# Three output tiles ahead of the last gate, and the first norm's squares on one engine

## The chip, the cores and the metric

The program runs on one core of a Trainium2 chip. The metric is the device time of one execution in microseconds (us), lower is better. The core's engines are named as in the profile: PE is TensorE's matmul, PEld its weight load, DVE is VectorE, ACT is ScalarE, POOL is GpSimd, and SP issues DMAs.

## The reference, cut to what matters

The program is a two-layer decoder trunk over 512 tokens of width 1024. Layer 0 has a recurrent block, layer 1 sparse attention; each is followed by a gated FFN with a small convolution. The change is in layer 0's recurrent block and in the norm before it:

```python
h = h + rglru_mixer(rmsnorm(h, lru_norm_g[j]), lru_w_in[j], ...)

def rmsnorm(x, g):
    y = x * lax.rsqrt(jnp.mean(x * x, axis=-1, keepdims=True) + EPS)
    return y * g

def rglru_mixer(x, w_in, conv_w, conv_b, gate_w, gate_b, a_param, w_out):
    y_br, x_br = jnp.split(x @ w_in, 2, axis=-1)      # each 1280 wide
    y_br = jax.nn.gelu(y_br)
    xc = causal_dwconv(x_br, conv_w, conv_b)          # width 4
    r_gate, i_gate = sigmoid(xc in 10 blocks of 128 @ gate_w + gate_b)
    a = jnp.exp(-LRU_C * r_gate * softplus(-a_param))
    b = sqrt(1 - a * a) * i_gate * xc
    h_t = a_t * h_(t-1) + b_t                         # a scan over tokens
    return (h * y_br) @ w_out
```

## The kernel before, in words

Activations lie with channels on the partitions and the 512 tokens along the row, so `x` is 8 tiles of 128x512 float32. Each matrix product is made of three matmuls (`mm3`, L214 to L216): an operand is split into a rounded high part and a low rest, and high by high, high by low and low by high are added up in one PSUM bank. The high half is made by ACT (a copy, `xh`, `whi`, `ch`, `hh`), the low half by DVE (a subtraction, `xl`, `wlo`, `cl`, `hl`). A weight tile is 128x1024 and 512 KB. Weight tile i goes through the pool `wx`, which has one buffer (tiles `wrawx`, `whix`, `wlox`), where i mod 3 is 2, and else through a pool with two buffers (`wraw`, `whi`, `wlo`). Loads and splits are asked for up to two tiles ahead.

The norm's row scale is applied late: the products run on `x * g`, and what comes out of PSUM is multiplied by `rbc`, the reciprocal root of the mean square, spread over the partitions. Its making has two steps on PE: `norm_finish` sums the squares over the partitions with float32 matmuls of one column (L276), DVE and POOL take the power (`nv`, `rtok`), and `norm_spread` broadcasts it by four more matmuls (L287), which ACT copies to `rbc`. In the kernel before the first three squares of the first norm are made and summed by POOL in a tile `ssum2` (L347, L349), the other five by ACT (L263, L266) and summed by DVE in `ssum` (L267); so `norm_finish` has eight matmuls there, against four in every other norm.

The recurrent block goes over ten blocks n of 128 channels. For each, `project(py, n)` and `project(px, n)` are 24 matmuls each; `yev(n)` and `conv(n)` empty their banks (both multiply by `rbc`); `conv(n)` makes `xr`, one ACT and three DVE taps into `xc`, and the halves `ch` and `cl`; `gate_mm(n)` is six matmuls on these, and `gate_act(n)` its sigmoids. Every two blocks a `burst` of exp, sqrt, gelu, scan and split follows and ends in `hh`, `hl`, the operands of the output product. `newacc` hands out six PSUM banks in turn, `newg` two.

The output product has eight tiles m, each with eight k of 24 matmuls from one weight tile (`lru_oa`) and two last k of six matmuls from a shared one (`lru_ob`). The last gate, `gate_mm(9)`, is tied behind the first short output tiles, which take only k = 0 to 5 until then and k = 6, 7 after it:

```python
            for m in range(2):
                po[m], first[m] = newacc(), self.w()
                outp(po[m], first[m], range(KA - 2))
            gate_mm(NB - 1, self.mm_name)
```

The order of the instructions on each engine comes from a scheduler, which goes by dependencies and priorities; weight splits and `conv` have a raised priority.

Of the kernel before, what the change touches and what calls it, by code (L numbers as in the profile page):

```python
# [10 lines left out]
F32 = mybir.dt.float32  # L11
# [6 lines left out]
NT = 512  # L18
KD = 8
NB = 10  # L20
# [4 lines left out]
RX = 2  # L25
WARM = 10
WLO, QLO, KLO, OLO = True, 'G', 'V', 'V'
KG = 3
NP = 9


# [33 lines left out]
CHP = 150  # L65

START = {1: (1, 0), 3: (0, 1), 4: (1, 1)}
KA, DEF = 8, 6
SLOPE = [2.0 ** (-0.5 * (h + 1)) for h in range(16)]


# [30 lines left out]
class Trunk:  # L102
# [166 lines left out]
    def norm_finish(self, newps):  # L269
        T, V = self.T, self.V  # L270
        ps = newps()
        parts = [self.ssum] + ([self.ssum2] if self.ssum2 is not None else [])
        self.ssum2 = None
        for t in range(4):
            for j, s in enumerate(parts):
                T.matmul(ps[:, t:t + 1], s[:, 128 * t:128 * t + 128], self.cst[:, C_ONE:C_ONE + 1],  # L276
                         start=(j == 0), stop=(j == len(parts) - 1))
        v = self.np_.tile([128, 4], F32, name="nv", bufs=1)
        V.tensor_scalar(v, ps[:, :4], 1.0 / 1024.0, 1e-6, op0=ALU.mult, op1=ALU.add)
        self.rtok = self.np_.tile([128, 4], F32, name="rtok", bufs=1)  # L280
        self.G.tensor_tensor(self.rtok, v, self.mhalf, op=ALU.pow)
# [11 lines left out]
    def start(self):  # L293
        nc, a = self.nc, self.a
        self.prm = self.cp.tile([128, P_END], F32, name="prm")
        self.cst = self.cp.tile([128, C_END], F32, name="cst")
        self.x = [self.cp.tile([128, NT], F32, name=f"x{k}") for k in range(KD)]
        self.plan()
        self.tins, self.tgrp, self.manual = [], None, False
        self.mhalf = self.cp.tile([128, 4], F32, name="mhalf")  # L300
        self.V.memset(self.mhalf, -0.5)
        warm = self.cp.tile([128, 4], F32, name="warm")
        self.S.activation(warm, self.mhalf, AF.Copy)
        self._dma(0)
        self._dma(1)
        self.wd = 2
        nc.scalar.dma_start(self.prm[:, :P_CW], a["prm"][:, :P_CW])
        self._half(0, 0, True)
        for k in range(KD):
            nc.sync.dma_start(self.x[k], a["x"][k])  # L310
            if k in START:
                self._half(*START[k], True)
        nc.sync.dma_start(self.cst, a["cst"])
        nc.sync.dma_start(self.prm[:, P_CW:], a["prm"][:, P_CW:])
        self.ident = self.cst[:, C_ID:C_ID + 128]
# [9 lines left out]
    def run(self):  # L325
        wx = ExitStack()
        extra = lambda: wx.enter_context(self.tc.tile_pool(name="wx", bufs=1))
        self.wx = extra()
        self.warm_up(WARM)
        self.start()  # L330
        st = self.stages
        g0 = {"lru": P_LRUG, "ffn0": P_FFNG, "nsa": P_NSAG, "ffn1": P_FFNG + 8}
        seq = [s for s in ("lru", "ffn0", "nsa", "ffn1") if s in st]
        self.norm_begin(g0[seq[0]])
        self.sq_eng = self.V
        self.ssum2 = self.np_.tile([128, NT], F32, name="rbc", bufs=1)
        for k in range(KD):
            self.norm_split(k)
            if k == 0:
                self._half(0, 0, False)  # L340
            if k in START:
                self._half(*START[k], False)
        self.wsp = 2
        for k in range(KD):
            if k < KG:
                sq = self.ssum2 if k == 0 else self.np_.tile([128, NT], F32, name="sq")
                self.G.tensor_mul(sq, self.x[k], self.x[k])  # L347
                if k > 0:
                    self.G.tensor_add(self.ssum2, self.ssum2, sq)  # L349
            else:  # L350
                self.norm_sq(k, k == KG)
        for s, nx in zip(seq, seq[1:] + [None]):
            self.next_g = g0[nx] if nx else P_FING
            self.next_split = nx is not None
            self.sq_eng = self.G if SSQ[seq.index(s)] else self.V
            if s == "lru":
                self.lru()
            elif s == "nsa":
                wx.close()
                self.spl = 1  # L360
                self.nsa()
                self.wx = extra()
                self.spl = 2
            else:
                self.ffn(int(s[-1]))
        if self.next_split or seq[-1][:3] != "ffn":
            for _ in self.final(slice(0, NT), self.ring(0, 1)):
                pass
        wx.close()
# [36 lines left out]
    def lru(self):  # L406
        S, V, G, T, prm = self.S, self.V, self.G, self.T, self.prm
        with ExitStack() as s:
# [4 lines left out]
            py, px, pg = {}, {}, {}  # L413
# [3 lines left out]
            def project(d, n):  # L417
                d[n] = newacc()
                self.proj(d[n], self.w(), self.xs, range(KD))

            def yev(n):
                y[n] = hp.tile([128, NT], F32R, name=f"hh{n}").bitcast(F32)
                V.tensor_mul(y[n], py[n], self.rbc)

            def conv(n):

                with self.tc.high_priority(offset=CHP):
                    conv_ops(n)
# [29 lines left out]
            def gate_mm(n, after=None):  # L458
                hi, lo = gw.pop(n)
                if n + 1 < NB:  # L460
                    gate_w(n + 1)
                pg[n] = []
                for j in range(2):
                    ps = newg()
                    sl = slice(128 * j, 128 * j + 128)
                    first = self.mm3(ps, hi[:, sl], lo[:, sl], *xcs[n], True, True)
                    if after:
                        self.tc.add_manual_dep(first, after, mybir.DependencyInfo(
                            mybir.DependencyClass.NoSync, mybir.DependencyReason.DATA), reason="output first")
                    pg[n].append(ps)  # L470

            def gate_act(n):
                r[n] = hp.tile([128, NT], F32R, name=f"hl{n}").bitcast(F32)
                ig[n] = p.tile([128, NT], F32, name="ig", bufs=6)
                self.tact(r[n], pg[n][0], AF.Sigmoid, bias=col(P_GB + n))
                self.tact(ig[n], pg[n][1], AF.Sigmoid, bias=col(P_GB + 10 + n))
                u[n] = p.tile([128, NT], F32, name="u", bufs=6)
                self.tact(u[n], r[n], AF.Tanh, scale=self.sp[:, 0, n:n + 1])
                self.G.tensor_mul(ig[n], ig[n], xc[n])
# [42 lines left out]
            def tick():  # L522
                if late:
                    for f in late.pop(0):
                        f()

            def burst(ns):
                at(0, lambda: exps(ns))
                at(1, lambda: sqrts(ns))
                at(2, lambda: gelus(ns))  # L530
                for j, n in enumerate(ns):
                    at(2 + j, lambda n=n: back1(n))
                    at(3 + j, lambda n=n: back2(n))
                    at(4 + j, lambda n=n: back3(n))
# [5 lines left out]
            for k in range(0, KD, 2):  # L540
                for d, w in ((py, w0), (px, w1)):
                    self.proj(d[0], tuple(t[:, 128 * k:128 * k + 256] for t in w), self.xs, range(k, k + 2))
            for n in range(NB):
                if n > 1:
                    project(py, n)
                if n > 0:
                    conv(n - 1)
                if n > 1:
                    gate_act(n - 2)
                    if n - 2 in last:  # L550
                        burst(last[n - 2])
                tick()
                if n > 0:
                    project(px, n)
                if n > 0:
                    gate_mm(n - 1)
                if n == 0:
                    self.norm_finish(newacc)
                    project(py, 1)
                    self.norm_spread(newacc)  # L560
                    self.sp = self.softplus(hp)
                    gate_w(0)
                yev(n)
                tick()

# [14 lines left out]
            po = {}  # L580

            def begin(m):
                po[m] = newacc()
                outp(po[m], self.w(), range(KA))


            first = {}
            for m in range(2):
                po[m], first[m] = newacc(), self.w()
                outp(po[m], first[m], range(KA - 2))  # L590
            gate_mm(NB - 1, self.mm_name)
# [1 line left out]
            burst(last[NB - 1])  # L593
            while late:
                tick()
            for m in range(2):
                outp(po[m], first[m], range(KA - 2, KA), 128 * (KA - 2))
            for m in range(2, DEF):
                begin(m)
            wo = []  # L600
            for m in range(KD):
# [691 lines left out]
```

## Time and profile before

| what | value |
|---|---|
| median of 3 runs | 1320.08 us (1318.04 to 1320.96) |
| profiled execution, its own time | 1320.14 us |
| its span, first to last instruction | 1318.3 us |
| PE busy | 1299.9 us, 99% of the span |
| DVE, ACT, POOL busy | 786.0, 611.4, 248.0 us |
| mean granted TensorE clock | 0.995 of full speed |

The profiled execution's own time is 1.8 us above its span; that part lies outside the instructions. A busy PE is one that has a matmul running: matmuls overlap, so the step from the start of one to the start of the next says more than their duration. The granted clock is 1.00 at 2.4 GHz and 0.50 at 1.2 GHz.

### The profile page before, as it was taken

The numbers are of one execution on the slowest core, as the hardware profiler recorded it, in microseconds if no ns is written. First come the engines' busy times: TensorE is split into PE (matmuls) and PEld (weight loads), VectorE is DVE, ScalarE is ACT, GpSimd is POOL, SyncE is SP. The second block draws the span as 40 slices with busy tenths as digits, with TensorE's granted clock in tenths as the row PEclk, the third lists the DMA queues.
The fourth block names the chain that finished last, engine by engine and source line by source line (L and its number), as shares of the span: only waits on it lengthen the run. The fifth ranks groups of instructions, "written<-read, shape, count | busy, mean of one in ns | idle before, by whom it ended". The sixth has DMA issues, their size and how long they took to land.

```text
span 1318.3 us, 16281 instructions
## 1 busy us (share of the span) xinstructions
PE 1299.9 (99%) x6166; PEld 1064.2 (81%) x6166; DVE 786.0 (60%) x1267; ACT 611.4 (46%) x980; POOL 248.0 (19%) x259
## 2 busy tenths in 40 slices
PE   8999999999999999999999999999999999999997
PEld 6888788888888888888787787888888888888886
DVE  7799765555555533336457978875655555542223
ACT  5789743333333322221348878865433333332220
POOL 2123331000000001115008567643000000000110
PEclk9999899999999999999999999999999999999999
DMA  7222222322222222224231100013222232223221
GB/s 239 91 75 101 77 84 97 98 97 100 96 99 99 98 90 92 94 78 141 96 112 33 34 33 33 17 46 115 97 96 96 96 96 96 96 96 97 96 80 64
DMA packets 36222, 117.71 MB, mean 89 GB/s; under 512 B 4144, under 2 KB 7728, under 8 KB 36144
## 3 DMA queue, kind: packets, MB, share of 16 engines
q1 hardware_dynamic: 34848, 115.61, 26.4%
q8 instruction: 48, 0.79, 0.2%
q10 hardware_dynamic: 1296, 1.07, 0.2%
q14 instruction: 30, 0.25, 0.1%
HBM read 114.57 MB, written 2.10 MB: 88 GB/s over the span
## 4 chain that ended last, share of the span: by engine, by line
PE 91%; DVE 3%; ACT 2%; issue 1%; POOL 1%; DMA 1%; SPq 0%; POOLq 0%; DVEq 0%; ACTq 0%
PE bank L215 27%; PE bank L214 27%; PE bank L216 27%; PE bank L1085 2%; PE bank L1105 1%; PE bank L1101 1%; PE bank L1031 1%; PE bank L1032 1%; PE bank L877 1%; PE bank L835 1%; PE bank L836 1%; PE bank L837 1%; DVE P L1044 0%; PE bank L1104 0%; ACT P L229 0%
## 5 line engine op out<-in xcount | busy, mean ns | idle before, releaser
L214 PE MATMUL bank<-xh,whi 128*128 128x512 f32 x760 | 297.8, 392 | 0.8 <-ACT xh L256 0.2
L215 PE MATMUL bank<-xl,whi 128*128 128x512 f32 x760 | 296.6, 390 | 1.6 <-DVE xl L257 1.6
L216 PE MATMUL bank<-xh,wlo 128*128 128x512 f32 x760 | 296.3, 390 | 1.0 <-DVE wlo L186 0.5
L185 ACT ACTIVATE whi<-wraw 128x1024 fp32r<-128x1024 f32 x143 | 151.2, 1058 | 307.7 <-PE bank L215 252.2
L186 DVE TENSOR_TENSOR wlo<-wraw,whi 128x1024 fp32r<-128x1024 f32 x133 | 164.0, 1233 | 130.5 <-ACT whi L185 120.2
L267 POOL TENSOR_TENSOR ssum<-ssum,sq 128x512 f32<-128x512 f32 x27 | 44.2, 1636 | 771.1 <-issue 581.1
L214 PEld LDWEIGHTS bank<-xh,whi 128*128 128x128 f32 x760 | 142.7, 188 | 33.1 <-DVE nm L1044 0.8
L216 PEld LDWEIGHTS bank<-xh,wlo 128*128 128x128 f32 x760 | 142.6, 188 | 31.8 <-DVE wlo L186 1.0
L215 PEld LDWEIGHTS bank<-xl,whi 128*128 128x128 f32 x760 | 142.7, 188 | 31.7 <-DVE xl L257 3.0
L185 ACT ACTIVATE whix<-wrawx 128x1024 fp32r<-128x1024 f32 x57 | 60.4, 1060 | 138.8 <-PE bank L215 137.2
L215 PE MATMUL bank<-xl,whix 128*128 128x512 f32 x296 | 116.5, 394 | 0.0
L214 PE MATMUL bank<-xh,whix 128*128 128x512 f32 x296 | 116.2, 393 | 0.0
L216 PE MATMUL bank<-xh,wlox 128*128 128x512 f32 x296 | 115.1, 389 | 0.0
L214 PE MATMUL bank<-fh,whi 128*128 128x512 f32 (+1 forms) x272 | 104.0, 382 | 0.0
L215 PE MATMUL bank<-fl,whi 128*128 128x512 f32 (+1 forms) x272 | 103.9, 382 | 0.0
L216 PE MATMUL bank<-fh,wlo 128*128 128x512 f32 (+1 forms) x272 | 103.9, 382 | 0.0
L1061 POOL TENSOR_SCALAR P<-P,c,gtok 128x512 f32<-128x512 f32 (+3 forms) x128 | 79.5, 635 | 100.6 <-DVE c L1057 86.0
L186 DVE TENSOR_TENSOR wlox<-wrawx,whix 128x1024 fp32r<-128x1024 f32 x57 | 69.7, 1222 | 42.5 <-ACT whix L185 42.4
L652 DVE TENSOR_TENSOR ar<-bank,rbc 128x512 f32<-128x512 f32 x48 | 33.2, 691 | 99.2 <-PE bank L216 99.2
L662 DVE TENSOR_TENSOR b<-bank,rbc 128x512 f32<-128x512 f32 x48 | 33.2, 691 | 86.1 <-PE bank L216 86.1
L229 ACT ACTIVATE P<-P,nm 128x512 f32<-128x512 f32 (+3 forms) x128 | 70.9, 556 | 16.8 <-DVE nm L1044 13.7
L229 ACT ACTIVATE t<-t 128x512 f32<-128x512 f32 x48 | 30.4, 632 | 98.0 <-DVE t L658 98.0
(224 smaller groups left out, 2322.8 us busy)
## 6 DMA issues: line engine op xcount, KB each, us to landing
wraw<-in_ffn_in_dram SPq DMA_DIRECT2D x65, 512.0 KB, 3.3
wraw<-in_ffn_out_dram SPq DMA_DIRECT2D x32, 512.0 KB, 3.3
wrawx<-in_ffn_in_dram SPq DMA_DIRECT2D x31, 512.0 KB, 3.2
wrawx<-in_ffn_out_dram SPq DMA_DIRECT2D x16, 512.0 KB, 3.2
wraw<-in_nsa_in_dram SPq DMA_DIRECT2D x16, 512.0 KB, 3.3
wraw<-in_lru_in_dram SPq DMA_DIRECT2D x12, 512.0 KB, 3.6
w<-in_cmp_w_dram SPq DMA_DIRECT2D x8, 512.0 KB, 4.9
wraw<-in_nsa_out_dram SPq DMA_DIRECT2D x8, 512.0 KB, 3.3
```

The lines of the kernel that those rows point to most:

```text
L185: self.S.activation(hi[:, c], raw[:, c], AF.Copy)
L186: (eng or (self.G if self.manual and WLO else self.V)).tensor_sub(lo[:, c], raw[:, c], hi[:, c].bitcast(F32))
L214: ins = mm(ps, wh, xh, start=first, stop=False)
L215: mm(ps, wh, xl, start=False, stop=False)
L216: end = mm(ps, wl, xh, start=False, stop=last)
L229: ins = self.S.activation(out, in_, func, **k)
L267: self.sq_eng.tensor_add(self.ssum, self.ssum, sq)
L652: V.tensor_mul(ar, pa, self.rbc)
L662: V.tensor_mul(b, pb, self.rbc)
L835: T.matmul(pv[t], xh[:, ts], hi[:, sl], start=(k == 0), stop=False)
L1061: G.tensor_scalar(Ps[g, i, br][r], Ps[g, i, br][r], st["c"][:, br, r:r + 1], gtok[:, i, gc:gc + 1], op0=ALU.mult, op1=ALU.mult)
L1085: T.transpose(st["t", kt][:, 128 * r:128 * r + 128], Ps[u][r][:, 128 * kt:128 * kt + 128], self.ident)
```

## The change

It has four parts. The load of weight tile 2 is issued ahead of the loads of `cst` and of the rest of `prm`. All eight squares of the first norm go to ACT and are summed by DVE in `ssum`. The start of the recurrent block is written out: the second `py` projection comes ahead of `norm_finish`, and the second `px` projection is cut in two halves of 12 matmuls with `norm_spread` between them; `gate_mm(0)` comes behind the third `py` projection. Three short output tiles stand ahead of the last gate in place of two, and seven whole ones ahead of the shared weights in place of six, the seventh in a bank of the gate's pair.

```diff
-KA, DEF = 8, 6
+KA, DEF, NE = 8, 7, 3
...
     def norm_finish(self, newps):
...
-        parts = [self.ssum] + ([self.ssum2] if self.ssum2 is not None else [])
-        self.ssum2 = None
         for t in range(4):
-            for j, s in enumerate(parts):
-                T.matmul(ps[:, t:t + 1], s[:, 128 * t:128 * t + 128], self.cst[:, C_ONE:C_ONE + 1],
-                         start=(j == 0), stop=(j == len(parts) - 1))
+            T.matmul(ps[:, t:t + 1], self.ssum[:, 128 * t:128 * t + 128], self.cst[:, C_ONE:C_ONE + 1],
+                     start=True, stop=True)
...
+        self._dma(2)
+        self.wd = 3
         nc.sync.dma_start(self.cst, a["cst"])
...
         for k in range(KD):
-            if k < KG:
-                sq = self.ssum2 if k == 0 else self.np_.tile([128, NT], F32, name="sq")
-                self.G.tensor_mul(sq, self.x[k], self.x[k])
-                if k > 0:
-                    self.G.tensor_add(self.ssum2, self.ssum2, sq)
-            else:
-                self.norm_sq(k, k == KG)
+            self.norm_sq(k, k == 0)
...
+            project(py, 1)
+            self.norm_finish(newacc)
+            px[1], w1 = newacc(), self.w()
+            self.proj(px[1], w1, self.xs, range(KD // 2))
+            self.norm_spread(newacc)
+            self.proj(px[1], tuple(t[:, 64 * KD:] for t in w1), self.xs, range(KD // 2, KD))
+            self.sp = self.softplus(hp)
+            gate_w(0)
+            yev(0)
+            tick()
+            conv(0)
+            yev(1)
+            tick()
+            for n in range(2, NB):
+                project(py, n)
+                if n == 2:
+                    gate_mm(0)
+                conv(n - 1)
...
             def begin(m):
-                po[m] = newacc()
+                po[m] = newg() if m == 6 else newacc()
                 outp(po[m], self.w(), range(KA))
...
-            for m in range(2):
+            for m in range(NE):
                 po[m], first[m] = newacc(), self.w()
                 outp(po[m], first[m], range(KA - 2))
             gate_mm(NB - 1, self.mm_name)
...
-            for m in range(2):
+            for m in range(NE):
                 outp(po[m], first[m], range(KA - 2, KA), 128 * (KA - 2))
-            for m in range(2, DEF):
+            for m in range(NE, DEF):
                 begin(m)
```

## Rows read from the trace of the kernel before

**Rows 1.** The page: busy time, share of the span and instructions.

```profile
PE 1299.9 (99%) x6166; PEld 1064.2 (81%) x6166; DVE 786.0 (60%) x1267; ACT 611.4 (46%) x980; POOL 248.0 (19%) x259
```

**Rows 2.** PE's waits: who waited for whom, total, times, longest.

```profile
PE bank L214 <- ACT ch L443: 1.9, 1, 1.9
PE bank L215 <- DVE xl L257: 1.6, 3, 0.7
```

**Rows 3.** PE's timeline around the last gate: start, us, instruction, idle before.

```profile
142.81 0.40 PE L216 MATMUL bank<-hh,wlo 128*128 128x512 f32 x1
145.10 0.77 PE L214 MATMUL bank<-ch,ghi 128*128 128x512 f32 x1 [1.90 <-ACT ch L443]
146.82 0.80 PE L215 MATMUL bank<-cl,ghi 128*128 128x512 f32 x1 [0.95 <-DVE cl L444]
...
152.30 0.40 PE L216 MATMUL bank<-hh,wlo 128*128 128x512 f32 x1
...
158.59 0.39 PE L216 MATMUL bank<-hh,wlo 128*128 128x512 f32 x1
```

**Rows 4.** Windows around it: busy time, then granted clock, DMA share, GB/s.

```profile
147.00:148.00 1.00, 1.00 (x3) 0.81 (x4) 1.00 (x1) 0.07 (x1) 0.90 (x1) 0.50 0.00 0
...
152.00:153.00 1.00, 1.00 (x6) 0.77 (x6) 0.41 (x1) 1.00 (x2) 0.00 (x0) 1.00 0.00 0
```

**Rows 5.** Groups of instructions, first 30 us: busy, mean ns of one, idle.

```profile
L257 DVE SCALAR_TENSOR_TENSOR xl<-x,prm,xh 128x512 fp32r<-128x512 f32 x8 | 8.5, 1088 | 1.1 <-ACT xh L256 1.0
...
L175 DVE TENSOR_TENSOR wlo<-wraw,whi 128x512 fp32r<-128x512 f32 x4 | 3.6, 893 | 2.9 <-ACT whi L174 2.9
...
L267 DVE TENSOR_TENSOR ssum<-ssum,sq 128x512 f32<-128x512 f32 x4 | 2.7, 680 | 0.0
```

**Rows 6.** DVE's timeline in the first 23 us.

```profile
9.71 3.47 DVE L257 SCALAR_TENSOR_TENSOR xl<-x,prm,xh 128x512 fp32r<-128x512 f32 x2
...
13.71 0.74 DVE L257 SCALAR_TENSOR_TENSOR xl<-x,prm,xh 128x512 fp32r<-128x512 f32 x1
...
19.71 1.22 DVE L186 TENSOR_TENSOR wlox<-wrawx,whix 128x1024 fp32r<-128x1024 f32 x1
```

**Rows 7.** DVE's timeline behind the last gate.

```profile
148.60 0.69 DVE L511 TENSOR_TENSOR hl<-u,hh 128x512 fp32r<-128x512 f32 x1 [0.15 <-ACT hh L510]
152.59 1.23 DVE L186 TENSOR_TENSOR wlox<-wrawx,whix 128x1024 fp32r<-128x1024 f32 x1 [3.30 <-ACT whix L185]
```

**Rows 8.** ACT's timeline behind the last gate.

```profile
151.50 1.06 ACT L185 ACTIVATE whix<-wrawx 128x1024 fp32r<-128x1024 f32 x1 [0.93 <-PE bank L215]
```

**Rows 9.** Chain that ended last: norm sums of the first and second norm.

```profile
20.78 1.68 PE bank L276 x16
...
203.73 0.79 PE bank L276 x8
```

**Rows 10.** POOL's timeline in the first 30 us.

```profile
9.21 3.43 POOL L349 TENSOR_TENSOR rbc<-rbc,sq 128x512 f32<-128x512 f32 x2
```

**Rows 11.** DVE's timeline in the next norm.

```profile
184.18 1.78 DVE L257 SCALAR_TENSOR_TENSOR xl<-x,prm,xh 128x512 fp32r<-128x512 f32 x1
```

**Rows 12.** POOL's timeline in the next norm.

```profile
183.17 3.94 POOL L267 TENSOR_TENSOR ssum<-ssum,sq 128x512 f32<-128x512 f32 x2 [0.60 <-ACT sq L266]
```

**Rows 13.** ACT's timeline in the first 23 us.

```profile
6.71 0.72 ACT L256 ACTIVATE xh<-x,prm 128x512 fp32r<-128x512 f32 x1 [1.62 <-DMA x<-in_x_dram]
...
17.61 0.64 ACT L266 ACTIVATE sq<-x 128x512 f32<-128x512 f32 x1 [1.90 <-DVE ssum L267]
18.15 1.04 ACT L185 ACTIVATE whix<-wrawx 128x1024 fp32r<-128x1024 f32 x1
```

**Rows 14.** ACT's timeline where the first norm's scale comes.

```profile
29.01 0.60 ACT L290 ACTIVATE rbc<-bank 128x512 f32<-128x512 f32 x1
```

**Rows 15.** DVE's timeline from there.

```profile
30.16 0.68 DVE L432 TENSOR_TENSOR xr<-bank,rbc 128x512 f32<-128x512 f32 x1
...
36.55 0.68 DVE L444 TENSOR_TENSOR cl<-xc,ch 128x512 fp32r<-128x512 f32 x1
```

More of the change, by code (lines that the diff above doesn't have):

```diff
@@ L27 @@
 WLO, QLO, KLO, OLO = True, 'G', 'V', 'V'
-KG = 3
 NP = 9
@@ L335, in run @@
         self.sq_eng = self.V
-        self.ssum2 = self.np_.tile([128, NT], F32, name="rbc", bufs=1)
         for k in range(KD):
@@ L542, in lru @@
                     self.proj(d[0], tuple(t[:, 128 * k:128 * k + 256] for t in w), self.xs, range(k, k + 2))
[L543 to L551, printed above, removed]
-                tick()
[L553 to L562, printed above, removed]
+            project(py, 1)
[16 more added lines that the diff above has]
+                conv(n - 1)
+                gate_act(n - 2)
+                if n - 2 in last:
+                    burst(last[n - 2])
+                tick()
+                project(px, n)
+                gate_mm(n - 1)
                 yev(n)
```

## The prediction

> **What bounds the kernel now.** I read the busy shares first. PE has a matmul running for nearly the whole span [rows 1], and the change keeps every 128x512 matmul, so it can win or lose only where PE stands still, runs slowly, or does something that goes away. The second view is PE's own waits [rows 2]. Two of the longest lie in places that the change touches: the wait for `ch` of the last gate, and those for `xl` in the first 14 us.
>
> The third view is PE's timeline around the last gate [rows 3]. From the matmul at 152.30 to the one at 158.59 there are 27 steps, so the pace of an unhindered stretch there is 0.233 us. From 142.81 to 152.30 there are 15 steps, which at that pace take 3.5 us; they took 9.49. So the gate costs 6.0 us. Of that, 2.06 us is the wait for `ch` (143.04 to 145.10) and 1.49 the wait for `cl` (145.33 to 146.82). The other 2.4 us are the clock: before the wait PE was continuously busy, and after it the granted clock is 0.50, the 1.2 GHz level, until about 152; then it is 1.00, 2.4 GHz [rows 4].
>
> The fourth view is the start. There PE is held by the splits of x, and DVE is the slow one: its eight `xl` average 1.09 us and its four first `wlo` 0.89 [rows 5], where an undisturbed `xl` takes 0.74 [rows 6] and an undisturbed tensor_tensor of that shape 0.68 [rows 5].
>
> **The change part by part.**
>
> *Third short tile.* It puts 6 x 3 = 18 matmuls more ahead of the last gate, 18 x 0.233 = 4.2 us. The gate's first matmul is then due at 143.04 + 4.2 = 147.24, its second, which needs `cl`, at 147.47. In the trace of before `ch` let PE go at 145.10 and `cl` at 146.82 [rows 3]. Both chains hang on the last `px` projection, which the change shifts as a whole, so I move everything together: `cl` comes 0.65 us before it is wanted, PE doesn't stop, and as it doesn't stop I expect no fall of the clock. All of the 6.0 us goes. If `cl` comes over 0.65 us later than now, a wait begins again.
>
> What is late next there: behind the gate, tile 0 takes k = 7 with `hl`, due at 147.24 + (6 + 3 + 1) x 0.233 = 149.57; DVE finished it at 148.60 + 0.69 = 149.29 [rows 7]. And the fourth tile's weights go into the one-buffer pool that tile 0 frees. Between the last use of `whix` and the fourth tile's first use of `wlox` PE now has 15 steps, 3.5 us; the last matmul's own 0.39, ACT's split of 1.06 [rows 8] and DVE's of 1.23 [rows 7] need 2.7. One more activation of some 0.7 us in front fits, two don't. Before, a whole tile of 24 matmuls lay there too. The seventh whole tile costs nothing: the same matmuls in another order, its bank freed by the last gate's first sigmoid about 20 us before it is wanted; the shared weights come one tile later in the same two buffers. The next norm then gets seven residuals close together and the eighth after 30 matmuls (7 us), in which DVE, ACT and POOL catch up.
>
> *Sums of the first norm.* Four matmuls of one column for eight. On the chain of waits the eight took 1.68 us, the four of the next norm 0.79 [rows 9]: 0.9 us less.
>
> *Squares off POOL.* While POOL's two sums ran (9.21 to 12.64, [rows 10]) DVE's two `xl` took 3.47 us; the one at 13.71, after POOL was through, took 0.74 [rows 6]. The same is seen far from the start's loads: in the next norm an `xl` took 1.78 [rows 11] under two sums on POOL [rows 12]. So I price what POOL takes from DVE at 8 x (1.088 - 0.74) + 4 x (0.893 - 0.68) = 2.8 + 0.85 = 3.6 us [rows 5]. DVE pays for it with three more sums, 3 x 0.68 = 2.0. Both are in the same queue ahead of the second `py` projection's `wlox`, so that comes 1.6 us sooner and PE with it: +1.6. Bounds: if DVE's instructions stay as slow as they were and the sums stand in front, -2.0; if all sums fall behind what PE wants, +3.6. I take the middle one, since in the trace sums of before stand on both sides of the last `xl`. ACT gets three more squares of 0.64, 1.9 us; it stood idle for 1.62 before the second `xh` and 1.90 before a later square [rows 13], so they fit and cost nothing; without those gaps they would delay `whix` (18.15, [rows 13]) by 1.9.
>
> The Trainium skill, "SBUF — State Buffer", section "SBUF: two separate sides", states that DVE and GpSimd share a port pair as an exclusive lock, that a DVE instruction with two SBUF inputs is shut out for the whole of a GpSimd instruction that reads SBUF, and that DMAs can't slow an engine's access. By that rule all of the 3.6 us comes back, and the sum is the one below. Were the loads to blame, nothing would come back, and the time would be that of the first rival. The durations above agree with the rule, but only a run without POOL's sums shows it.
>
> *Order of the start and the earlier load.* The norm's sums now come 24 matmuls later, so three more DVE sums ahead of them cost nothing there: these 24 at PE's pace are over 5 us. The load of weight tile 2 ahead of `cst` and `prm` costs nothing: `cst` is first wanted by the norm's sums, which are later now, and ACT's split of that tile had no wait for its load [rows 13]. Two new covers are thin. The third `py` projection takes the bank that `yev(0)` empties, and `rbc` comes ahead of only 12 matmuls (2.8 us): ACT's copy is 0.60 [rows 14], then `xr` and `yev` on DVE, 0.68 each, together 2.0; a weight split of DVE (1.2) in front makes it late by 0.4. The first gate has 36 matmuls (8.4 us) after `norm_spread`; from the copy's start at 29.01 to the end of `cl` at 36.55 + 0.68 it took 8.2 [rows 14, 15]. For these and the two covers behind the last gate I set 0.5 us of new waits in all, an estimate between 0 and 1.5.
>
> **The sum.** 6.0 + 0.9 + 1.6 - 0.5 = 8.0 us. The profiled execution's own time is 1320.1, its span 1318.3; the median of the runs is 1320.1 too, so the time becomes 1320.1 - 8.0 = 1312.1, the span about 1310.3.
>
> **The rivals.**
>
> *The start gives nothing back (chance 0.20).* DVE is as slow as before for another reason, or the scheduler puts squares and sums ahead of `wlox`. Against it speak the 0.74 and 1.78 above. For it: a square had to wait 1.90 us for DVE's sum, with `whix` queued behind it [rows 13]. Start at -2.0: 6.0 + 0.9 - 2.0 - 0.5 = 4.4, so 1315.7. The Trainium skill, "TensorE: Matmul & The Clock Gate", section "Architectural detail", says of ACT and DVE that they are strict FIFO; the split behind the waiting square is such a case.
>
> *The last gate still waits (0.10).* DVE's and ACT's order between 135 and 147 us changes, and `cl` comes 2.1 us later than now, 1.5 after it is wanted. If the clock falls as it did, 1.5 + 2.4 of the 6.0 stay: 8.0 - 3.9 = 4.1, so 1316.0.
>
> *Slower (0.05).* ACT and DVE fall into lockstep in the start: `xh`, square, sum, `xl` one after another for each of the eight tiles, as the squares have two buffers and all their sums are now in DVE's queue. A round is 0.72 + 0.64 + 0.68 + 0.74 = 2.8 us [rows 5, 6, 13]; seven rounds from 6.71 end at 26.2, six matmuls later (27.6) the first projections are through, against 20.6 now (0.2 before the chain's sums at 20.78 [rows 9]). That is 7.0 us lost, with the clock's 2.4 on top 9.4, against 6.0 + 0.9 - 0.5 = 6.4 won: 1323.1. It decides once the first projections end 6.4 us later than now, or 4.0 if the clock falls too. Against it: the square that waited longest comes after the last `xh` was made.
>
> That the third tile isn't ahead of the gate at all is excluded: the gate is tied to the last matmul emitted before it, which is the third tile's.
>
> **How the numbers follow.** Forecast 0.62, the three rivals 0.20, 0.10 and 0.05, anything else 0.03. The predicted time is the forecast's, 1312.1. The range goes down to 1309.6 (start +3.6, no new waits: 10.5) and up to 1316.7 (start -2.0 and 1.5 of new waits: 3.4), which takes in the first two rivals. A measurement of this kernel tells about 0.2%, 2.6 us, from no change. The forecast and the first two rivals are all faster than that; leaving room for two of them at once: faster 0.89, same 0.06, slower 0.05.
>
> **What would show it right or wrong.** Last gate: no idle PE ahead of `gate_mm(9)`, granted clock 1.00 throughout 135 to 160, its first matmul at about 144.7 (147.24 - 0.9 - 1.6). Start: `xl` at 0.74 each, the sums in DVE's queue behind most of them, the first projections through near 19; the norm's sums x8 on the chain. If the `xl` stay above 1 us, my pricing of POOL is wrong; if PE waits for `wlox` or for `yev(0)`, that of the order. A clock of 0.50 anywhere before 200 us would break the sum by about 2.4.

## The result, and the profile after

| | median us (runs) | lowest to highest | profiled: own time, span | ratio to before |
|---|---|---|---|---|
| before | 1318.66 (6) | 1318.04 to 1320.96 | 1320.1, 1318.3 | |
| after | 1310.63 (6) | 1309.84 to 1311.32 | 1311.32, 1309.5 | 0.9936 [0.9923, 0.9949] |
| after, run again | 1312.74 (5) | 1310.18 to 1313.6 | 1310.18, 1308.3 | 0.9954 [0.9941, 0.9966] |

The change makes the kernel faster, by 8.0 us (0.6%) in the first series and by 6.1 in the second (there the kernel before had 1318.8, median of 21 runs). 1312.1 had been predicted. The executions of one kernel differ by some us, and in the kernel before with its clock: of its 51 in three later series, the 12 with a mean granted clock of 0.994 took 1319.6 to 1321.0 us, the 13 with 0.997 took 1317.2 to 1318.9.

Of the kernel after, first the page's busy shares, then all of PE's waits between 4 and 205 us, which are one row (who waited for whom, total, times, longest):

```profile
PE 1295.0 (99%) x6158; PEld 1062.5 (81%) x6158; DVE 787.2 (60%) x1270; ACT 612.8 (47%) x983; POOL 242.2 (18%) x254
```

```profile
PE bank L214 <- DVE xl L256: 0.3, 1, 0.3
```

PE has 4.9 us less to do than in [rows 1], and its matmul records are eight fewer: those of the norm's sums. The 1.6 us of waits for `xl` [rows 2] are down to 0.3, and no wait for `ch` or `cl` is left anywhere.

The last gate, in PE's timeline of the kernel after (start, duration, instruction; no row has idle time before it), and the windows around it (busy time of PE, PEld, DVE, ACT, POOL, then granted clock, DMA share, GB/s):

```profile
143.13 0.39 PE L215 MATMUL bank<-hh,wlo 128*128 128x512 f32 x1
143.36 0.40 PE L213 MATMUL bank<-ch,ghi 128*128 128x512 f32 x1
143.60 0.39 PE L214 MATMUL bank<-cl,ghi 128*128 128x512 f32 x1
...
148.95 0.40 PE L213 MATMUL bank<-hh,whix 128*128 128x512 f32 x1
```

```profile
140.00:146.00 6.00, 6.00 (x28) 4.83 (x27) 5.23 (x6) 3.07 (x4) 1.56 (x1) 1.00 0.00 1
146.00:152.00 6.00, 6.00 (x28) 4.81 (x27) 4.02 (x3) 5.97 (x7) 1.75 (x1) 1.00 0.26 87
```

Against [rows 3] both waits are gone, and against [rows 4] the 0.50 too: the clock is granted in full. How thin the cover is shows DVE's timeline of the same stretch:

```profile
142.21 0.67 DVE L435 TENSOR_TENSOR cl<-xc,ch 128x512 fp32r<-128x512 f32 x1
142.79 1.78 DVE L502 TENSOR_TENSOR hl<-u,hh 128x512 fp32r<-128x512 f32 x1
144.73 0.69 DVE L502 TENSOR_TENSOR hl<-u,hh 128x512 fp32r<-128x512 f32 x1 [0.15 <-ACT hh L501]
147.68 1.22 DVE L185 TENSOR_TENSOR wlox<-wrawx,whix 128x1024 fp32r<-128x1024 f32 x1 [2.26 <-ACT whix L184]
```

`cl` is there at 142.88 and wanted at 143.60: 0.7 us to spare, where the prediction had 0.65. The last `hl` ends at 145.42 and is wanted 0.3 later; `wlox` of the fourth tile ends at 148.90, and its first user is the third matmul from 148.95, at 149.41.

The start: DVE's groups of the first 30 us (busy, mean ns of one, idle), and the norm sums on the chain that ended last:

```profile
L256 DVE SCALAR_TENSOR_TENSOR xl<-x,prm,xh 128x512 fp32r<-128x512 f32 x8 | 5.9, 748 | 1.1 <-ACT xh L255 1.1
L266 DVE TENSOR_TENSOR ssum<-ssum,sq 128x512 f32<-128x512 f32 x7 | 4.8, 687 | 0.1
L174 DVE TENSOR_TENSOR wlo<-wraw,whi 128x512 fp32r<-128x512 f32 x4 | 2.8, 689 | 3.2 <-ACT whi L173 3.2
```

```profile
23.50 0.79 PE bank L272 x8
...
193.85 0.79 PE bank L272 x8
```

The eight `xl` take 748 ns where they took 1088, the `wlo` 689 for 893 [rows 5]. The first norm's sums take 0.79 us for 1.68, and the second norm's begin at 193.85, 9.88 earlier than in [rows 9].

**A measure that two runs share.** In the traces ACT's third `xh` starts anywhere between 6.74 and 8.42 us, in whichever kernel, as the first loads of x land sooner or later. So I cut each run in four by three instants: x, the start of ACT's third `xh`; g, the first `ch` matmul of the last gate but one, which waits in no run; s, the second norm's sums on the chain. What lies between x and g is the start, between g and s the last gate, from s to the end of the span the rest. All from the traces:

```
                    x       g       s     span    g-x    s-g   span-s
before            8.00  133.25  203.73  1318.3  125.25  70.48  1114.6
after             7.77  129.37  193.85  1309.5  121.60  64.48  1115.7
after again       7.34  128.91  193.36  1308.3  121.57  64.45  1114.9
tiles only        7.50  132.74  197.20  1311.3  125.24  64.46  1114.1
start only        7.17  128.92  198.61  1314.6  121.75  69.69  1116.0
squares only      7.58  130.32  201.02  1317.1  122.74  70.70  1116.1
order only        7.98  133.07  202.80  1317.8  125.09  69.73  1115.0
no early load     8.42  130.93  195.45  1311.4  122.51  64.52  1116.0
POOL back         6.95  132.12  196.58  1311.9  125.17  64.46  1115.3
half cover        7.31  128.88  195.35  1310.2  121.57  66.47  1114.9
no seventh        6.93  128.52  194.50  1308.9  121.59  65.98  1114.4
filler            6.74  132.66  201.25  1315.9  125.92  68.59  1114.7
```

The change takes 3.65 us out of the start and 6.0 out of the gate, 9.65 in all. The rest is 1.1 longer in this pair of profiles; over the twelve it lies between 1114.1 and 1116.1. Three things make most of that up. PE's wait for `w` of the compression weights (L873, a DMA) is 0.5 us before, 0 after, and 0 to 1.3 in the other profiles. Behind PE's last column sums, the last broadcast of the kernel after fell into a half clock (it took 0.71 us before),

```profile
1300.38 1.22 PE L387 MATMUL bank<-cst,frt 128*128 128x128 f32 x4 [1.03 <-POOL frt L383]
```

and SyncE waited longer for the last output to land, first before, then after:

```profile
SPq L1288 <- DMA out_dram<-x: 1.8, 1, 1.8
...
SPq L1284 <- DMA out_dram<-x: 3.2, 1, 3.2
```

This last wait follows an edit. It is 1.8 in all four kernels that leave the first norm's squares as they were (before, tiles only, order only, filler) and 2.4 to 3.2 in all eight that have them on ACT. So 0.6 to 1.4 us of what the change wins seem to go again at the end. By what way, no run shows.

### The profile page after: what moved, and what is told of

Same layout as the page of the kernel before. It is cut to its first block, busy times and chain, and to the rows that moved or that the text cites. A ratio compares the mean times of both kernels' runs of the same rounds, so it can differ in the third digit from the quotient of the medians.

```text
span 1309.5 us, 16269 instructions
## 1 busy us (share of the span) xinstructions
PE 1295.0 (99%) x6158; PEld 1062.5 (81%) x6158; DVE 787.2 (60%) x1270; ACT 612.8 (47%) x983; POOL 242.2 (18%) x254
## 4 chain that ended last, share of the span: by engine, by line
PE 94%; DVE 2%; ACT 1%; issue 1%; POOL 1%; DMA 0%; SPq 0%; POOLq 0%; DVEq 0%; ACTq 0%
PE bank L213 28%; PE bank L214 28%; PE bank L215 27%; PE bank L1081 2%; PE bank L1101 1%; PE bank L1097 1%; PE bank L873 1%; PE bank L1027 1%; PE bank L1028 1%; PE bank L832 1%; PE bank L831 1%; PE bank L833 1%; DVE P L1040 0%; PE bank L1100 0%; ACT P L228 0%
```

## The experiments

Medians, with the kernel before on the same chip:

| run | us | before | ratio |
|---|---|---|---|
| tiles only | 1313.65 | 1318.8 | 0.9964 [0.9951, 0.9976] |
| start only | 1315.99 | 1318.8 | 0.9981 [0.9972, 0.9989] |
| squares only | 1317.98 | 1318.8 | 0.9994 [0.9985, 1.0003] |
| order only | 1319.43 | 1318.46 | 1.0005 [0.9996, 1.0014] |
| no early load | 1312.07 | 1318.46 | 0.9950 [0.9937, 0.9962] |
| POOL back | 1313.56 | 1318.79 | 0.9964 [0.9951, 0.9978] |
| half cover | 1311.71 | 1318.79 | 0.9949 [0.9934, 0.9964] |
| no seventh | 1312.25 | 1318.79 | 0.9952 [0.9940, 0.9965] |
| filler | 1317.88 | 1318.79 | 0.9993 [0.9984, 1.0002] |

**The change once more**, unedited, beside the others.

> The changed kernel a second time. Theory: its landmarks repeat (fourth output tile 9.9 us earlier than before, first projections through at 17.8), and the time is 8 to 10 us below before. In its first profile the span shrank by only 8.8, though the last norm's first matmul came 10.7 earlier: the last output load landed 1.4 us later and a half-clock stretch added 0.5. Theory: these two vary from run to run and a second profile shows a span nearer 10 us below. Rival: they belong to the change and repeat.

1312.74 us: 2.1 above the first series, though its own profile agrees with the first to 0.03 us in both parts. The median is 6.1 below before, not the expected 8 to 10; the span of the profiled execution is 10.0 below, but that was the fastest of the five (1310.18, the slowest 1313.6). Of the two things that were expected to vary, the half clock of the last broadcast does (0.93 us here); the later landing came again (2.7), as the rival has it. The changed kernel's two medians are 2.1 apart, so the reading below goes by the parts in the table, and by medians only where they differ by more.

**Tiles only**: the kernel before with the three tiles and the seventh, the start untouched.

```diff
-KA, DEF = 8, 6
+KA, DEF, NE = 8, 7, 3
...
-                po[m] = newacc()
+                po[m] = newg() if m == 6 else newacc()
...
```

> Only the output part: three short tiles, seven whole ones; start and norm as before. Theory: the last gate doesn't wait, clock 1.00 there, 6.0 us less than before; the start's waits stay. Rival: the gate's cover holds only with the faster start, some 1 to 4 of the 6.0 us stay as a wait and a half clock.

The start is as before (125.24), the gate 6.0 shorter (64.46), and PE waits for neither `ch` nor `cl`: the cover holds without the faster start. The time is 5.1 lower.

**Start only**: the changed kernel with two short tiles, and no seventh.

```diff
-KA, DEF, NE = 8, 7, 3
+KA, DEF, NE = 8, 6, 2
...
-                po[m] = newg() if m == 6 else newacc()
+                po[m] = newacc()
```

> Only the start: squares on ACT, order, earlier load; two short tiles and six whole ones as before. Theory: first projections through 2.8 us earlier, norm's sums 0.9 less, so 3.7 us less than before, and the gate still costs 6.0 with its half clock. Rival: the gains of the two parts are not additive, and the wait for the gate grows or shrinks by over 0.5 us.

The start is 3.5 shorter, and the time 2.8 lower, where 3.7 was expected. The gate's two waits are back, in PE's timeline:

```profile
140.77 0.50 PE L213 MATMUL bank<-ch,ghi 128*128 128x512 f32 x1 [1.89 <-ACT ch L434]
142.50 0.50 PE L214 MATMUL bank<-cl,ghi 128*128 128x512 f32 x1 [1.22 <-DVE cl L435]
```

The gate costs 5.2 here (69.69 - 64.46), not 6.0, more than the 0.5 by which the rival would have it change. The waits are the same, but the clock falls later and for less long, as the windows show (columns as above):

```profile
143.00:144.00 1.00, 1.00 (x5) 0.69 (x4) 1.00 (x1) 0.38 (x1) 0.58 (x1) 0.77 0.09 16
...
145.00:146.00 1.00, 1.00 (x3) 0.77 (x3) 0.00 (x0) 0.99 (x2) 0.00 (x0) 0.50 0.00 0
...
147.00:148.00 1.00, 1.00 (x6) 0.82 (x5) 0.61 (x1) 0.93 (x2) 0.00 (x0) 1.00 0.00 0
```

Order only has the same (5.3) with a start as long as before, so it needn't come from the faster start.

**Squares only**: the kernel before with all squares on ACT and all sums on DVE.

```diff
-        self.ssum2 = self.np_.tile([128, NT], F32, name="rbc", bufs=1)
+        self.ssum2 = None
...
-            if k < KG:
...
-            else:
-                self.norm_sq(k, k == KG)
+            self.norm_sq(k, k == 0)
```

> Before, with all squares of the first norm on ACT and summed by DVE, order of the projections and load as before. Theory: without POOL's work each xl takes 0.75 us, the first projections end near 17.9, but the norm's sums then stand behind DVE's last sum (19.5) and PE waits 1 to 2 us: 1.5 to 3 us less than before in all. Rival: the start's gain comes from the new order and the earlier load, so xl stay near 1.1 us or the projections still end near 20.5, and only the 0.9 us of the sums is won, or less.

`xl` is at 750 ns, and the start is 2.5 us shorter (125.25 to 122.74). The norm's sums themselves begin only 0.87 earlier (19.91 for 20.78), but five matmuls of the third projection already stand ahead of them. The time falls by 0.8 only, which its interval doesn't tell from nothing: the gate is as dear as ever in this profile (70.70), the wait for `w` is 1.2 where it was 0.5 before, and that for the last landing 2.6 where it was 1.8. What is left of DVE's lateness is one wait, in PE's timeline (the first row is the last matmul of the first projections), and in ACT's and then DVE's its cause:

```profile
17.37 0.39 PE L216 MATMUL bank<-xh,wlo 128*128 128x512 f32 x1
...
18.95 0.50 PE L216 MATMUL bank<-xh,wlox 128*128 128x512 f32 x1 [0.53 <-DVE wlox L186]
```

```profile
16.05 0.63 ACT L266 ACTIVATE sq<-x 128x512 f32<-128x512 f32 x1 [1.03 <-DVE ssum L267]
16.59 1.04 ACT L185 ACTIVATE whix<-wrawx 128x1024 fp32r<-128x1024 f32 x1
...
17.67 1.23 DVE L186 TENSOR_TENSOR wlox<-wrawx,whix 128x1024 fp32r<-128x1024 f32 x1
```

The split of weight tile 2 stands in ACT's queue behind a square that waits 1.03 us for DVE's sums, as in [rows 13].

**POOL back**: the changed kernel, and POOL does five operations on the x tiles, into a tile that nobody reads.

```diff
+        idle = self.np_.tile([128, NT], F32, name="rbc", bufs=1)
+        for k in range(3):
+            self.G.tensor_mul(idle, self.x[k], self.x[k])
+            if k > 0:
+                self.G.tensor_add(idle, idle, self.x[k])
```

> The changed kernel plus five POOL instructions on x in the start (three squares, two sums) whose result nobody reads; ACT and DVE do what they do in the changed kernel. Theory (DVE is slowed by POOL): the xl average 1.0 us or more again, the first projections end 2 to 3.6 us later than the 17.6 to 17.8 of the changed kernel, and so does everything behind. Rival (the slow xl came from the loads at that time, or from the order): xl stay at 0.75 and the projections end below 18.

DVE's groups of the first 30 us:

```profile
L256 DVE SCALAR_TENSOR_TENSOR xl<-x,prm,xh 128x512 fp32r<-128x512 f32 x8 | 7.9, 1002 | 0.2 <-ACT xh L255 0.2
L266 DVE TENSOR_TENSOR ssum<-ssum,sq 128x512 f32<-128x512 f32 x7 | 5.9, 839 | 0.1
L174 DVE TENSOR_TENSOR wlo<-wraw,whi 128x512 fp32r<-128x512 f32 x4 | 3.8, 955 | 2.8 <-ACT whi L173 2.8
```

DVE's same instructions take 8 x 0.254 + 7 x 0.152 + 4 x 0.266 = 4.2 us more, PE waits 2.7 for `xl`, and the start is 125.17: 3.6 longer than after. Nothing but POOL's running differs, and all that the start had won is gone. (That it is as long as before again is partly chance: here DVE also makes all the sums of the squares.)

**Order only**: the kernel before with the new order of the start and the early load of weight tile 2; squares and sums as before.

```diff
+        self._dma(2)
+        self.wd = 3
...
+            project(py, 1)
+            self.norm_finish(newacc)
+            px[1], w1 = newacc(), self.w()
...
```

> The kernel before with the new order of the start (norm sums wanted behind the third projection, weight tile 2 loaded ahead of the constants) and nothing else: the first three squares stay on POOL, the sums of two parts, two short tiles ahead of the last gate. Theory (POOL's squares are what holds the start): PE still waits about 2 us for xl and wlo, xl stays near 1.09 us on average, the sixteen column sums stay; at most the wait for wlox and the stall around the first gate go, so the start gains 0 to 1 us: PE comes to the wait of the last gate at 142.2 to 143.2 (143.20 before), time 1317.5 to 1318.8 where the kernel before has 1318.8. Rival (the order carries the start's gain): PE comes there at 141.2 or sooner, time 1316.5 or less. Together with the run that has only the squares moved and the one that has both, it gives each part's share and whether the shares add up.

The start is 125.09: 0.16 shorter, and PE still waits 1.9 for `xl` and 0.5 for `wlo`. With POOL's squares in place the order is worth nothing that these profiles can tell: the median is 1.0 above that of before (its interval holds no change), and two profiles of one start can lie 0.7 apart (before and filler). (The gate costs 5.3, again with a shorter fall of the clock.)

**No early load**: the changed kernel without the two lines of the early load.

```diff
-        self._dma(2)
-        self.wd = 3
```

> The changed kernel with weight tile 2 loaded where it was loaded before, behind the constants. Theory (prediction: the earlier load costs and gives nothing): whix of that tile is still split before PE wants it, no wait of PE for whix or wlox before 24 us, first matmul of the last gate at 143.4 within 0.5, time as the changed kernel's, 1310.6 to 1312.7. Rival (the earlier load is part of the gain, since the split of that tile now comes 3 us sooner): PE waits for whix or wlox 0.5 us or more ahead of 20 us, and all behind it comes as much later: 1311.5 to 1313.5.

The rival has it: PE waits, and the start is 0.9 longer (122.51 for 121.60). It lies between the end of the first projections (10.1 us after x in both) and the norm's sums. In the time this doesn't show, 1312.07 beside 1310.63 and 1312.74. First PE's row of it and ACT's two, then ACT's of the kernel after:

```profile
19.77 0.50 PE L215 MATMUL bank<-xh,wlox 128*128 128x512 f32 x1 [0.53 <-DVE wlox L185]
```

```profile
16.88 0.63 ACT L265 ACTIVATE sq<-x 128x512 f32<-128x512 f32 x1 [1.03 <-DVE ssum L266]
17.41 1.05 ACT L184 ACTIVATE whix<-wrawx 128x1024 fp32r<-128x1024 f32 x1
```

```profile
15.10 1.05 ACT L184 ACTIVATE whix<-wrawx 128x1024 fp32r<-128x1024 f32 x1
16.22 0.64 ACT L265 ACTIVATE sq<-x 128x512 f32<-128x512 f32 x1
17.02 0.63 ACT L265 ACTIVATE sq<-x 128x512 f32<-128x512 f32 x1 [0.16 <-DVE ssum L266]
```

The earlier load doesn't bring data that someone waited for; it changes the order in ACT's queue. With it the split stands ahead of the square that waits, without it behind.

**Half cover**: the changed kernel with three of the third tile's first six k ahead of the gate, so 9 matmuls less.

```diff
-                outp(po[m], first[m], range(KA - 2))
+                outp(po[m], first[m], range(KA - (2 if m < 2 else 5)))
...
```

> The changed kernel with half of the third short tile, three k of six, ahead of the last gate: 9 matmuls, 2.1 us less cover. Theory: ch is just in time, cl 1.4 us late; if a wait of that length leaves the clock alone the gate costs 1.4 more than in the changed kernel, if it falls 1.4 plus up to 2.4. Rival: the cover of the changed kernel has more to spare than 0.65 us, and less than 1 us is lost.

The wait is back for `cl` alone, in PE's timeline, but the clock isn't lost (windows below):

```profile
140.77 0.45 PE L213 MATMUL bank<-ch,ghi 128*128 128x512 f32 x1
142.44 0.50 PE L214 MATMUL bank<-cl,ghi 128*128 128x512 f32 x1 [1.22 <-DVE cl L435]
```

```profile
138.00:144.00 6.00, 4.78 (x20) 3.28 (x18) 5.96 (x6) 1.59 (x3) 2.29 (x2) 1.00 0.01 1
144.00:150.00 6.00, 5.96 (x26) 4.56 (x26) 3.29 (x4) 5.95 (x8) 1.76 (x1) 1.00 0.08 16
```

From g to s it is 2.0 longer: 1.4 at `cl`, the rest at the `hl` behind it. By medians it can't be told from the changed kernel.

**No seventh**: the changed kernel with six tiles ahead instead of seven.

```diff
-KA, DEF, NE = 8, 7, 3
+KA, DEF, NE = 8, 6, 3
...
```

> The changed kernel with six whole tiles ahead of the shared weights, as before, and three short ones. Theory: the third short tile alone carries the gain at the gate; the same time as the changed kernel within 0.5 us by landmarks. Rival: the seventh tile is worth something (or costs), 1 us or more.

The rival has it: from g to s it is 1.5 longer, with a wait of PE that the changed kernel doesn't have:

```profile
166.43 0.50 PE L214 MATMUL bank<-hl,whix 128*128 128x512 f32 x1 [1.08 <-DVE hl L502]
```

**Filler**: the kernel before with 16 matmuls ahead of the last gate whose result nobody reads, in the place of the third tile.

```diff
+            pad = self.pp.tile([128, NT], F32, name="bank1")
+            for j in range(16):
+                i = T.matmul(pad, first[0][0][:, :128], hy[0][0], start=True, stop=True)
+                self.mm_name = getattr(i, "ins", i).name
```

(The last line ties the gate behind the filler.)

> Before, with 16 matmuls on data that is there, into a bank that nobody reads, between the two short tiles and the last gate: PE is kept busy for 16 x 0.233 = 3.7 us of work that does nothing. Theory: the wait for ch and cl is covered and the clock stays at 1.00 through 160 us, so the gate costs 3.7 in place of 6.0, about 2.3 less than before. Rival: the clock falls for another reason (what runs at the gate itself), then the gate costs the filler and 2.4 more, and nothing is won.

PE's timeline and the windows:

```profile
142.45 3.91 PE L593 MATMUL bank<-hh,whix 128*128 128x512 f32 x16
146.19 0.40 PE L214 MATMUL bank<-ch,ghi 128*128 128x512 f32 x1
146.43 0.40 PE L215 MATMUL bank<-cl,ghi 128*128 128x512 f32 x1
```

```profile
140.00:146.00 6.00, 6.00 (x28) 4.81 (x27) 5.96 (x6) 2.19 (x4) 2.76 (x3) 1.00 0.00 0
146.00:152.00 6.00, 6.00 (x26) 4.40 (x25) 3.59 (x4) 4.61 (x6) 1.73 (x2) 1.00 0.01 1
```

No wait at the gate, no fall of the clock, and the gate costs 4.1 (68.59 - 64.46) instead of 6.0, though it does no more useful work than before: the filler takes 3.7, and four steps of PE at the `hl` behind the gate take 0.4 more than at its pace. So keeping the clock up gives back 1.9 us net. It isn't the whole price of the clock, since the filler is 0.2 longer than the waits that it fills. Only the part between g and s is read here; its start is 0.7 longer than that of before, with the same code there and x landing 1.3 us sooner, so that instant x compares less well for it.

## Why the prediction was right

**The last gate, 6.0: right, in mechanism and size.** Tiles only gives 6.0 by itself. The split into 3.5 us of waits and 2.4 of clock holds: without the waits the clock doesn't fall (filler, after), nor with the second alone (half cover); with both of them it does. The 2.4 is one draw, though: with the same waits it is 1.7 us in start only and order only (5.2 and 5.3, less 3.5) and 2.7 in squares only (6.2). The cover needed was priced right too: `cl` 0.65 us to spare, measured 0.7; with nine matmuls, 2.1 us, less, a wait of 1.4 (half cover).

**Norm sums, 0.9: right**, 1.68 to 0.79.

**Squares off POOL, 3.6 - 2.0 = 1.6: right in size, by a path that differs.** Squares only shortens the start by 2.5, which is 0.9 of sums and 1.6. Counted from x, `wlox` of weight tile 2 starts 1.6 sooner there than before (17.67 - 7.58 for 19.71 - 8.00), as the prediction has it. But the kernel before doesn't wait for that `wlox`; what holds it are the `xl` [rows 2]. With these gone the first projections end 10.0 us after x instead of 12.6, so the extra sums cost nothing there; only then does PE come to `wlox` too early, and lose part of it again. POOL back, which brings only POOL's work back, costs 3.6. The rival that the start gives nothing back is refuted by both, and so is the lockstep of ACT and DVE: first projections through at 17.8 us, against 20.6 before and "near 19" in the prediction. The Trainium skill, "SBUF — State Buffer", section "SBUF: two separate sides", says that of a GpSimd instruction that reads SBUF and a DVE one with two SBUF inputs the first to start holds their ports and the other waits, and that loads don't slow an engine; POOL back agrees, with the same loads and 1.00 us for 0.75 per `xl`.

**Order and early load, 0: this step was wrong.** It says that the load of weight tile 2 "costs nothing", and looked only for costs. They are worth 1.1 of the start's 3.65, and only once POOL's squares are gone: 0.16 alone (order only), 0.2 for the order (squares only to no early load, 122.74 to 122.51), and 0.9 for the load (to 121.60). The 0.16 and the 0.2 are hardly more than the profiles of one start differ by (five of the new one, 121.57 to 121.75); the 0.9 is clear of that. The cause was in [rows 13] and named in the first rival: a split queued behind a square that waits for DVE's sums. I took this as a danger to the new start and didn't see that the edits could lift it. In the kernel before it costs PE nothing yet; with the squares off POOL it costs the 0.9. The Trainium skill, "TensorE: Matmul & The Clock Gate", section "Architectural detail", calls ACT strictly in order; the wait of `wlox` behind the square is what that looks like here (0.53 in two runs without the early load, 0 in those with it, POOL's squares being gone).

**The seventh tile, "costs nothing": a gap.** It costs nothing, but leaving it out costs 1.5. With three tiles ahead PE gets through the gate 6 us sooner, and DVE's chain behind the last gate doesn't: without the tile PE waits 1.08 for `hl`, so I read the tile as the cover for it. The change has the tile, so the sum isn't touched; without it I would have been 1.5 off.

**New thin covers, -0.5: none measured**, inside its bounds of 0 to 1.5. `gate_mm(0)`, `yev(0)` and the two covers behind the last gate all run without a wait.

**The end: not in the sum.** The wait for the last output is 0.6 to 1.4 us longer in every kernel with the squares on ACT. The prediction looked no further than the second norm.

**The sum.** Its own terms, put right, are 6.0 + 0.9 + 1.6 + 1.1 = 9.6 against the 9.65 that the traces show from x to s; 8.0 was predicted. That the medians are just 8.0 apart in the first series is partly chance: what the sum missed, 1.6, is offset by the end and by the base. I subtracted from 1320.1, the time of one profiled execution; in four series, 6 to 21 runs of before each, the medians of that kernel are 1318.5 to 1318.8. So a gain read against that execution is some 1.4 more than the medians show. An estimate from these figures: 9.65 less 0.6 to 1.4 less 1.4 leaves 6.9 to 7.7, between the 8.0 and the 6.1 of the two series. The time of 1312.1 is 1.5 above the first series and 0.6 below the second. The signatures followed: the gate's first matmul came at 143.36 instead of 144.7, 1.3 sooner, and x had landed 0.2 sooner. Why the second series shows 6.1 where its profile shows the same 9.65 is not settled: its profile is that of its fastest execution, and the parts that vary by run (x, the clock's fall before, the wait for `w`, the end) are together as large as the difference.

## What to carry to other kernels

Price an edit at the start of a kernel by what it does to the order of each engine's queue, also where it only moves a load: a weight split one place further back, behind an instruction that waits, cost PE 0.5 us of waiting and the start 0.9. A cover that makes PE come sooner to the next dependence needs the next cover with it; look at what the same chain delivers last, here `hl` behind the gate. And when two profiles of one kernel differ by a load's landing, measure from an instant behind it: the parts of the changed kernel then agreed to 0.03 us where the two spans differ by 1.2. Measure what is left too: there the change lost some of its gain.

## What the runs showed that I had not expected

- Gains that need each other: taking the squares off POOL shortens the start by 2.5 us, the order with its load by 0.16, both together by 3.5 to 3.65.
- A gap of 1.2 us in PE's work left the granted clock at 1.00 (half cover); 1.9 and then 1.2 with one matmul between took it to 0.50, for some 3.5 us (start only, order only) or nearly 7 (before, squares only). What decides the length these runs don't show.
- The start of ACT's third `xh` moved over 1.7 us between profiles. The stretch behind the second norm moved by 2.0 with no edit to it, and its last wait, for the landing of the output, is longer wherever the first norm's squares are on ACT.
